# Attention starts with the values' product, and exponential, gelu and the routing's scores are issued later

## The chip, the cores and the metric

The kernel runs on one core of a Trainium2 chip. The metric is the device time of one execution in microseconds. Each engine (TensorE or PE, VectorE or DVE, ScalarE or ACT, GpSimd or POOL, SyncE or SP) takes its own instructions in the order in which the program issued them, so an instruction that waits holds up all that is queued behind it on its engine.

## What is computed

Two residual blocks on 256 tokens of width 2048, all in float32. The first block is a gated MLP with mixing over tokens and then a stick-breaking attention; the second a convolution and mLSTM mixer and then a layer of routed experts (PEER). The change touches the start of the attention and the experts:

```python
def stick_breaking_branch(xn, w_in, w_out):
    proj = xn @ w_in
    q, k, v, zg = jnp.split(proj, 4, axis=-1)
    ...
def peer_ffn(h, wq, keys, u, v):
        q = (xt @ wq).reshape(-1, PEER_HEADS, 2, PEER_HALF)
        s = jnp.einsum('thpc,hpnc->thpn', q, keys)
        sv, si = lax.top_k(s, PEER_TOPK)
        ...
        top_s, top_j = lax.top_k(cand, PEER_TOPK)
        gate = jax.nn.softmax(top_s.astype(jnp.float32), axis=-1)
        act = jax.nn.gelu(jnp.einsum('thkd,td->thk', ue, xt).astype(jnp.float32), approximate=False)
        return jnp.einsum('thk,thkd->td', (gate * act).astype(xt.dtype), ve)
```

The kernel takes the product with all 16384 rows of `u` and of `v`; the routing gives a mostly zero matrix of gates, scattered into DRAM, that the gelu values are multiplied by.

## The kernel before

**Weights.** Every product streams its weights. `Stream` loads 1 MB tiles (`raw`, three buffers, L108, on SP's queue) and splits each half of a tile into a high part `wh` (a copy on ACT, recorded at L194, six buffers) and a low part `wl` (a subtraction on DVE, L131, five buffers). `next` (L147) hands out one half and issues the copies and subtractions that lie some halves ahead. A low part is so issued four halves before TensorE needs it, and a high part five. Here a *half-block* is the TensorE work on one half of a weight tile: 12 matmuls in `gemm` (L328; lines 341 to 343), 8 pairs in `gemm_t` (L379; lines 393 and 395). The stages one after the other are the gated MLP, the attention, the mixer, the products with `wq`, those with `u` (L1283, 32 units of 4 blocks, each block two half-blocks) and those with `v`.

**Background tasks.** All that isn't a large product is written as generators. `bg.step` advances every task to its next `yield`, once per half-block, and `bg.finish` runs named tasks to their end at once. So a `yield` sets the place of an instruction in its engine's order: it moves what follows by one half-block.

**The start of the attention.** `prep` (L612), one task for each quarter of the hidden state, transposes it (L623) and splits it on ACT and DVE (L630). The last quarter's task also works out the reciprocal norm (`rms_rstd`) and then calls `rows` (L597), which spreads it along a row with two small products (diagonals at L601 on DVE, matmuls at L604). `P3` (L245) sets the order of the products: keys, values, queries, gate for the first group. The keys' first block asks for the quarters one by one, the last of them in the middle of its second half-block.

**Routing.** `route` (L1159) runs four times, one after the other, while the `wq` and then the `u` products go on. For each it transposes the queries (L408), copies them on ACT (`qT`, L194), yields twice, and multiplies by the keys (L1172, for `t` 0 and 1); then come two rounds of top-16 on DVE (L1147 to L1151, L1186 to L1205), the subtraction of the maximum (L1210, DVE), the exponential (ACT, with its own table), a yield, the rest of the softmax (L1213 to L1215) and the `scatter` (L1221): 256 indirect DMAs in all on POOL's queue (L1226). The next `route` issues its transposes at the step after the exponential of `t` 1.

**The products with u.** After each block DVE adds the two parts of the accumulator (L1289), and after every second block ACT applies gelu to two of them; after four blocks a DMA on SP writes the unit to DRAM (L1294). `first_v` and `prep_v` (L1257) fetch gates and gelu values of the first units, multiply them (L1263, L1265) and split them for the products with `v` when the last units of `u` run.

Of the kernel before, what the change touches and what calls it, by code (L numbers as in the profile page):

```python
# [8 lines left out]
AF = mybir.ActivationFunctionType  # L9
# [160 lines left out]
def _block(ctx, tc, A, out):  # L170
    nc = tc.nc
# [15 lines left out]
    def act(out, in_, func, **kw):  # L187

        if func not in (AF.Copy, AF.Identity, AF.Abs, AF.Square):
            if func in SETS:  # L190
                table_for(func)
            else:
                table[0] = func
        S.activation(out, in_, func, **kw)  # L194
# [8 lines left out]
    def ft(i, shape, dt=F32):  # L203

        return _view(sb.tile([P, 1024], dt, name=nm(f"f{i}"), tag=f"f{i}"), shape)
# [7 lines left out]
    def rot(group, slots):  # L213
        i = turn.get(group, 0)
        turn[group] = i + 1
        return slots[i % len(slots)]
# [25 lines left out]
                add_w("awo", n, [c - 1])  # L242
    for n in range(4):
        add_w("awo", n, [7])
    P3 = [(w, g) for g in range(2) for w in "kvqz"] + [(w, g) for g in (2, 3) for w in "kvq"] + [("z", 2), ("z", 3)]  # L245
    for w, g in P3:
        add_w("bwi", "qkvz".index(w) * 4 + g, range(4))
    for n in range(4):
# [127 lines left out]
        bg.step()  # L376
        return r

    def gemm_t(x, evac, need=()):  # L379


        acc = pp.tile([P, 512], F32, name=nm("acc"), tag=f"acc{rot('acct', (0, 1))}", bufs=2)
        lo = acc[:, 0:T].rearrange("p (c h) -> p c h", h=2)
        both = acc.rearrange("p (a c h) -> p a c h", a=2, h=2)
        for half in range(2):
            if half:
                bg.step()
            wh, wl = st.next()
            for k in range(8):
                if k % 4 == 0 and need:  # L390
                    bg.finish(need[2 * half + k // 4])
                m = x[half][:, k].rearrange("p (h a c) -> p a c h", h=2, a=2)
                E.matmul(both, wh[:, k * P:(k + 1) * P], m, start=half == 0 and k == 0, stop=False,  # L393
                         skip_group_check=True)
                E.matmul(lo, wl[:, k * P:(k + 1) * P], m[:, 0], start=False, stop=half == 1 and k == 7,  # L395
                         skip_group_check=True)
        evac(acc)
        bg.step()
# [345 lines left out]

    first = True
    for w, g in P3:
        need = [p1tasks[i] for i in range(4)] if first else []
        first = False
        if w == "v":
            d = ft(2, [2, 512])  # L750
            qkv[w, g] = d

            def ev(acc, d=d):
                for t in range(2):
                    V.tensor_scalar(d[:, t], acc[t], r1[:, t:t + 1], None, op0=ALU.mult)
            gemm(x1h, x1l, FULL, ev)
            continue
        d = ft({"q": (0, 0, 0, 3), "k": (1, 1, 1, 6), "z": (3, 6, 0, 1)}[w][g], [4, T])
        for b in range(4):
            def ev(acc, b=b):  # L760
                o = d[:, b].rearrange("p (h c) -> p c h", h=2)
                V.tensor_reduce(o, acc.rearrange("p (a c h) -> p c h a", a=2, h=2),
                                axis=mybir.AxisListType.X, op=ALU.add)
                V.tensor_tensor(d[:, b], d[:, b], rrow[:, 1 if w == "q" else 0], op=ALU.mult)
                if w == "z" and b % 2:
                    act(d[:, b - 1:b + 1], d[:, b - 1:b + 1], AF.Silu)
            gemm_t(xb, ev, need if b == 0 else [])
        if w == "z":
            ytask[g] = bg.add(y3_chain(g, d))
            continue  # L770
        qkv[w, g] = d
        if w == "q":
            atask[g] = bg.add(attn_group(g))
# [385 lines left out]
    def route(n, q, before):  # L1159

        yield from wait(before)
        qT = ft(2, [4, T])

        def dst(pr, p):
            act(qT[:, 2 * pr:2 * pr + 2], p.rearrange("p (k t) -> p k t", k=2), AF.Copy)
        transpose4(lambda t, j: q[:, t, j * P:(j + 1) * P], dst)
        yield
        yield
        for t in range(2):
            p = ps()  # L1170
            for hp in range(4):
                E.matmul(p[:, hp * P:(hp + 1) * P], qT[:, hp, t * P:(t + 1) * P], keysT[:, 4 * n + hp],  # L1172
                         start=True, stop=True)
            s = et(rot("s7", (0, 1)), [4, P])
            act(s, p.rearrange("p (h n) -> p h n", h=4), AF.Copy)
            yield
            ws = ft(rot("rw", (3, 6)), [1024])
            sv = ws[:, 0:64].rearrange("p (a b) -> p a b", a=4)
            si = ws[:, 64:128].bitcast(U32).rearrange("p (a b) -> p a b", a=4)
            sif = ws[:, 128:192].rearrange("p (a b) -> p a b", a=4)  # L1180
            yield from paced([op for hp in range(4) for op in topk16(s[:, hp], sv[:, hp], si[:, hp])], 4)
            V.tensor_copy(sif, si)
            for hh in range(2):
                head = 2 * n + hh
                cand = et(rot("cand", (2, 3)), [16, 16])
                V.tensor_tensor(cand, sv[:, 2 * hh][:, :, None].to_broadcast([P, 16, 16]),  # L1186
                                sv[:, 2 * hh + 1][:, None, :].to_broadcast([P, 16, 16]), op=ALU.add)
                wo = 256 + hh * 256
                tj = ws[:, wo + 16:wo + 32].bitcast(U32)
                yield from paced(topk16(cand.rearrange("p a b -> p (a b)"), tvs[:, t, head], tj), 2)  # L1190
                ab = ws[:, wo + 32:wo + 64].bitcast(U32).rearrange("p (a b) -> p a b", a=2)
                V.tensor_scalar(ab[:, 0], tj, 4, None, op0=ALU.logical_shift_right)
                V.tensor_scalar(ab[:, 1], tj, 15, None, op0=ALU.bitwise_and)
                abf = ws[:, wo + 64:wo + 96].rearrange("p (a b) -> p a b", a=2)
                key = ws[:, wo + 96:wo + 128].rearrange("p (a b) -> p a b", a=2)
                V.tensor_copy(abf, ab)
                for s_ in range(2):
                    oh = et(rot("oh", (4, 5)), [16, 16])
                    V.tensor_tensor(oh, abf[:, s_][:, :, None].to_broadcast([P, 16, 16]),
                                    C("iota")[:, None, 0:16].to_broadcast([P, 16, 16]), op=ALU.is_equal)  # L1200
                    V.tensor_tensor(oh, oh, sif[:, 2 * hh + s_][:, None, :].to_broadcast([P, 16, 16]),  # L1201
                                    op=ALU.mult)
                    V.tensor_reduce(key[:, s_], oh, axis=mybir.AxisListType.X, op=ALU.add)
                V.scalar_tensor_tensor(key[:, 0], key[:, 1], float(P), key[:, 0], op0=ALU.mult, op1=ALU.add)
                V.tensor_scalar(idx[:, t, head * 16:(head + 1) * 16], key[:, 0], float(P), C("pidx"),  # L1205
                                op0=ALU.mult, op1=ALU.add)
                yield
            hs = slice(2 * n, 2 * n + 2)
            ex, es = gat[:, t, hs], ws[:, 192:194]
            V.tensor_tensor(ex, tvs[:, t, hs], tvs[:, t, hs, 0:1].to_broadcast([P, 2, 16]), op=ALU.subtract)  # L1210
            act(ex, ex, AF.Exp)
            yield
            V.tensor_reduce(es, ex, axis=mybir.AxisListType.X, op=ALU.add)  # L1213
            V.reciprocal(es, es)
            V.tensor_tensor(ex, ex, es[:, :, None].to_broadcast([P, 2, 16]), op=ALU.mult)  # L1215
            if n == 0:
                scatter(n, [t])
        if n:
            scatter(n, range(2))
# [53 lines left out]
    def first_v():  # L1273
        yield from wait(rts[-1])
        while len(done_u) < NU - 4:
            yield
        load_v(0)
        while len(done_u) < NU - 1:
            yield
        load_v(1)  # L1280
        yield from prep_v(0)

    done_u = set()  # L1283
    fv = bg.add(first_v())
    for u in range(NU):
        a = ft(rot("act", (0, 1)), [4, T])
        for b in range(4):
            def ev(acc, b=b):
                V.tensor_reduce(a[:, b].rearrange("p (h c) -> p c h", h=2),  # L1289
                                acc.rearrange("p (a c h) -> p c h a", a=2, h=2), axis=mybir.AxisListType.X, op=ALU.add)  # L1290
                if b % 2:
                    act(a[:, b - 1:b + 1], a[:, b - 1:b + 1], AF.Gelu)
            gemm_t(x3, ev)
        nc.sync.dma_start(out=Ad[u], in_=a)  # L1294
        done_u.add(u)
    bg.finish(fv)
    bg.drain()

# [135 lines left out]
```

## Time and profile before

| | us |
|---|---|
| median of 3 runs (3077.58 to 3080.34) | 3079.38 |
| the profiled execution | 3076.71 |
| its span in the profile | 3074.9 |
| PE busy in it | 3007.0 (98%) |
| DVE busy | 2028.9 (66%) |
| ACT busy | 1469.3 (48%) |
| POOL busy | 471.8 (15%) |

The profile names for each instruction its engine, line, and output and input tiles; an idle stretch before it is put down to the instruction that ended it. The granted clock is TensorE's, as a share of full speed. Idle time of TensorE is what the span could lose; idle time of another engine matters only where TensorE waits for it.

### The profile page before, as it was taken

The numbers are of one execution on the slowest core, as the hardware profiler recorded it, in microseconds if no ns is written. First come the engines' busy times: TensorE is split into PE (matmuls) and PEld (weight loads), VectorE is DVE, ScalarE is ACT, GpSimd is POOL, SyncE is SP. The second block draws the span as 40 slices with busy tenths as digits, with TensorE's granted clock in tenths as the row PEclk, the third lists the DMA queues.
The fourth block names the chain that finished last, engine by engine and source line by source line (L and its number), as shares of the span: only waits on it lengthen the run. The fifth ranks groups of instructions, "written<-read, shape, count | busy, mean of one in ns | idle before, by whom it ended". The sixth has DMA issues, their size and how long they took to land.

```text
span 3074.9 us, 39571 instructions
## 1 busy us (share of the span) xinstructions
PE 3007.0 (98%) x15488; PEld 2670.8 (87%) x15488; DVE 2028.9 (66%) x2704; ACT 1469.3 (48%) x1622; POOL 471.8 (15%) x275
## 2 busy tenths in 40 slices
PE   8999999998999999999999999999999999999997
PEld 7888888887999987888888888899999888888886
DVE  6565556666666676656558999855556766666666
ACT  5454444444554555545444444544444444444443
POOL 0000000000000000000001668888830000000001
PEclk9999999999999999999999999999999999999999
DMA  7776666665666575666656677878776988888874
GB/s 276 246 255 214 219 221 216 225 211 188 195 200 206 190 247 194 203 205 207 229 187 206 185 198 201 235 226 232 222 252 237 320 275 274 283 286 287 272 259 153
DMA packets 230603, 702.33 MB, mean 228 GB/s; under 512 B 50576, under 2 KB 144912, under 8 KB 158864
## 3 DMA queue, kind: packets, MB, share of 16 engines
q1 hardware_dynamic: 192912, 697.57, 66.7%
q0 software_dynamic: 37504, 2.25, 2.8%
q8 instruction: 121, 1.98, 0.2%
q14 instruction: 66, 0.54, 0.1%
HBM read 647.18 MB, written 52.56 MB: 228 GB/s over the span
## 4 chain that ended last, share of the span: by engine, by line
PE 88%; DVE 8%; ACT 2%; issue 1%; DMA 0%; SPq 0%; DVEq 0%; ACTq 0%
PE acc L393 16%; PE acc L341 13%; PE acc L342 13%; PE acc L343 13%; PE acc L395 8%; PE y L343 7%; PE y L342 7%; PE y L341 7%; DVE wl L131 3%; ACT e L194 1%; DVE f L1289 0%; PE ms L562 0%; PE ms L408 0%; DVE f L1151 0%; DVE e L1201 0%
## 5 line engine op out<-in xcount | busy, mean ns | idle before, releaser
L131 DVE TENSOR_TENSOR wl<-raw,wh 128x1024 fp32r<-128x1024 f32 x1106 | 1342.0, 1221 | 600.6 <-PE acc L342 262.9
L194 ACT ACTIVATE wh<-raw 128x1024 fp32r<-128x1024 f32 x1106 | 1159.8, 1056 | 1157.2 <-PE acc L343 511.5
L393 PE MATMUL acc<-xs,wh 128*128 128x512 f32 x2816 | 932.5, 385 | 0.0
L395 PE MATMUL acc<-xs,wl 128*128 128x256 f32 x2816 | 770.0, 273 | 3.5 <-DVE wl L131 3.5
L1226 POOL DMA_INDIRECT Gd<-f x256 | 455.5, 1779 | 1795.5 <-DVE f L1215 1672.3
L341 PE MATMUL acc<-wh,xs 128*128 128x512 f32 x1728 | 664.3, 384 | 13.4 <-ACT wh L194 9.3
L342 PE MATMUL acc<-wl,xs 128*128 128x512 f32 x1728 | 657.3, 380 | 0.5 <-DVE wl L131 0.5
L343 PE MATMUL acc<-wh,xs 128*128 128x512 f32 x1728 | 657.0, 380 | 0.0
L393 PEld LDWEIGHTS acc<-xs,wh 128*128 128x128 f32 x2816 | 535.1, 190 | 74.5 <-DVE xs L630 0.2
L395 PEld LDWEIGHTS acc<-xs,wl 128*128 128x128 f32 x2816 | 543.1, 193 | 4.2 <-DVE wl L131 4.1
L341 PE MATMUL y<-wh,xs 128*128 128x512 f32 x1024 | 388.1, 379 | 0.0
L342 PE MATMUL y<-wl,xs 128*128 128x512 f32 x1024 | 388.1, 379 | 0.0
L343 PE MATMUL y<-wh,xs 128*128 128x512 f32 x1024 | 388.1, 379 | 0.0
L341 PEld LDWEIGHTS acc<-wh,xs 128*128 128x128 f32 x1728 | 328.1, 190 | 62.9 <-ACT wh L194 9.3
L343 PEld LDWEIGHTS acc<-wh,xs 128*128 128x128 f32 x1728 | 327.8, 190 | 47.1 <-DVE xs L837 0.4
L342 PEld LDWEIGHTS acc<-wl,xs 128*128 128x128 f32 x1728 | 328.2, 190 | 46.7 <-DVE wl L131 1.0
L343 PEld LDWEIGHTS y<-wh,xs 128*128 128x128 f32 x1024 | 193.5, 189 | 27.5
L341 PEld LDWEIGHTS y<-wh,xs 128*128 128x128 f32 x1024 | 193.5, 189 | 27.5
L342 PEld LDWEIGHTS y<-wl,xs 128*128 128x128 f32 x1024 | 193.5, 189 | 27.4
L1289 DVE TENSOR_REDUCE f<-acc 128x256 f32<-128x512 f32 x128 | 88.5, 691 | 107.7 <-PE acc L395 107.6
L194 ACT ACTIVATE f<-f 128x512 f32<-128x512 f32 (+1 forms) x80 | 47.2, 591 | 225.0 <-DVE f L1289 162.4
L1314 POOL TENSOR_TENSOR res<-res,xs 128x512 f32<-128x512 f32 x6 | 9.7, 1645 | 801.0 <-DVE res L1311 801.0
(219 smaller groups left out, 1715.8 us busy)
## 6 DMA issues: line engine op xcount, KB each, us to landing
raw<-in_pu_dram SPq DMA_DIRECT2D x128, 1024.0 KB, 4.9
raw<-in_pv_dram SPq DMA_DIRECT2D x128, 1024.0 KB, 5.4
raw<-in_bwi_dram SPq DMA_DIRECT2D x64, 1024.0 KB, 4.9
raw<-in_w_dram SPq DMA_DIRECT2D x56, 1024.0 KB, 5.4
Gd<-zero SPq DMA_DIRECT2D x64, 512.0 KB, 6.9
raw<-in_aw_u_dram SPq DMA_DIRECT2D x32, 1024.0 KB, 5.7
raw<-in_aw_z_dram SPq DMA_DIRECT2D x32, 1024.0 KB, 5.8
raw<-in_awo_dram SPq DMA_DIRECT2D x32, 1024.0 KB, 5.8
```

The costliest lines, as they stand in the source:

```text
L131: self.nc.vector.tensor_tensor(l, raw[:, j * 1024:(j + 1) * 1024], self.hi[q].bitcast(F32), op=ALU.subtract)
L194: S.activation(out, in_, func, **kw)
L341: E.matmul(o, a, wa, start=first and opens, stop=False)
L342: E.matmul(o, a, wb, start=False, stop=False)
L343: E.matmul(o, b, wa, start=False, stop=fin and closes)
L393: E.matmul(both, wh[:, k * P:(k + 1) * P], m, start=half == 0 and k == 0, stop=False, skip_group_check=True)
L395: E.matmul(lo, wl[:, k * P:(k + 1) * P], m[:, 0], start=False, stop=half == 1 and k == 7, skip_group_check=True)
L1226: nc.gpsimd.indirect_dma_start(out=Gd[t][hh].rearrange("e c -> (e c)")[:, None], out_offset=bass.IndirectOffsetOnAxis(ap=idx[:, t, at:at + ...
L1289: V.tensor_reduce(a[:, b].rearrange("p (h c) -> p c h", h=2), acc.rearrange("p (a c h) -> p c h a", a=2, h=2), axis=mybir.AxisListType.X, ...
L1314: (nc.gpsimd if t == 0 or n in (1, 2) else V).tensor_tensor(v, v, gb[1][:, (n - 1) * 512:n * 512], op=ALU.add)
```

## The change

Three edits. First, in group 0 the values' product comes before the keys', and as it is a `gemm`, each quarter of the hidden state is asked for a quarter of that product (two half-blocks) later than the one before. Second, in the routing four yields instead of two stand between the copies of `qT` and the first scores, and five yields between the subtraction L1210 and the exponential. Third, in the products with `u` each gelu is held back and issued at the end of the next block, ahead of that block's own addition; the DMA that stores the unit and the mark that the unit is done go with the last one.

```diff
-    P3 = [(w, g) for g in range(2) for w in "kvqz"] + [(w, g) for g in (2, 3) for w in "kvq"] + [("z", 2), ("z", 3)]
+    P3 = [(w, 0) for w in "vkqz"] + [(w, 1) for w in "kvqz"] + [(w, g) for g in (2, 3) for w in "kvq"] + [("z", 2), ("z", 3)]
...
-                if k % 4 == 0 and need:
-                    bg.finish(need[2 * half + k // 4])
...
-        need = [p1tasks[i] for i in range(4)] if first else []
+        need = {i: [p1tasks[i]] for i in range(4)} if first else {}
...
-            gemm(x1h, x1l, FULL, ev)
+            gemm(x1h, x1l, FULL, ev, need)
...
-            gemm_t(xb, ev, need if b == 0 else [])
+            gemm_t(xb, ev)
...
         transpose4(lambda t, j: q[:, t, j * P:(j + 1) * P], dst)
-        yield
-        yield
+        for _ in range(4):
+            yield
...
             V.tensor_tensor(ex, tvs[:, t, hs], tvs[:, t, hs, 0:1].to_broadcast([P, 2, 16]), op=ALU.subtract)
+            for _ in range(5):
+                yield
             act(ex, ex, AF.Exp)
...
+    owed = []
+
+    def settle():
+        while owed:
+            owed.pop(0)()
+
     for u in range(NU):
         a = ft(rot("act", (0, 1)), [4, T])
+
+        def leave(u=u, a=a):
+            act(a[:, 2:4], a[:, 2:4], AF.Gelu)
+            nc.sync.dma_start(out=Ad[u], in_=a)
+            done_u.add(u)
+
         for b in range(4):
-            def ev(acc, b=b):
+            def ev(acc, b=b, a=a, leave=leave):
+                settle()
                 V.tensor_reduce(a[:, b].rearrange("p (h c) -> p c h", h=2),
                                 acc.rearrange("p (a c h) -> p c h a", a=2, h=2), axis=mybir.AxisListType.X, op=ALU.add)
-                if b % 2:
-                    act(a[:, b - 1:b + 1], a[:, b - 1:b + 1], AF.Gelu)
+                if b == 1:
+                    owed.append(lambda: act(a[:, 0:2], a[:, 0:2], AF.Gelu))
+                elif b == 3:
+                    owed.append(leave)
             gemm_t(x3, ev)
-        nc.sync.dma_start(out=Ad[u], in_=a)
-        done_u.add(u)
+    settle()
     bg.finish(fv)
     bg.drain()
```

## Rows read from the trace of the kernel before

**Rows 1.** TensorE's waits, whole span: waiter, its releaser: us in total, times, longest.
```profile
PE ms L1172 <- ACT f L194: 14.5, 3, 5.2
...
PE ms L604 <- DVE e L601: 7.6, 1, 7.6
...
PE acc L395 <- DVE wl L131: 3.5, 2, 1.8
```

**Rows 2.** Stretches: bounds, length, PE, PEld, DVE, ACT, POOL busy, clock, DMA, GB/s.
```profile
1690.00:1960.00 270.00, 252.04 (x1521) 230.82 (x1519) 251.87 (x638) 123.49 (x141) 198.29 (x113) 0.97 0.71 197
1960.00:2395.00 435.00, 435.00 (x2656) 400.07 (x2657) 262.17 (x262) 202.78 (x214) 253.23 (x147) 1.00 0.78 238
2395.00:3050.00 655.00, 655.00 (x3036) 573.58 (x3035) 417.71 (x357) 296.28 (x284) 0.00 (x0) 1.00 0.80 274
```

**Rows 3.** The same view, the stretches right after TensorE's four long idle times.
```profile
1715.20:1720.40 5.20, 5.17 (x19) 4.72 (x20) 3.69 (x8) 3.79 (x5) 3.62 (x3) 0.50 0.76 208
...
1798.60:1802.30 3.70, 3.70 (x15) 3.43 (x16) 2.31 (x3) 3.70 (x5) 1.67 (x2) 0.54 1.00 324
...
1881.20:1884.30 3.10, 3.09 (x12) 2.91 (x13) 1.68 (x2) 3.10 (x5) 2.79 (x2) 0.51 0.75 217
...
715.30:720.30 5.00, 5.00 (x17) 4.45 (x18) 1.16 (x4) 1.72 (x3) 0.00 (x0) 0.50 0.06 23
```

**Rows 4.** Timeline, DVE and PE, start of the attention: start, duration, instruction, [idle before].
```profile
710.28 1.22 DVE L131 TENSOR_TENSOR wl<-raw,wh 128x1024 fp32r<-128x1024 f32 x1
...
714.87 0.48 DVE L601 TENSOR_SCALAR e<-con,rstd 128x128 f32<-128x128 f32 x2
...
715.30 1.19 PE L604 MATMUL ms<-e,con 128*128 128x128 f32 x4 [7.59 <-DVE e L601]
```

**Rows 5.** ScalarE's waits from 1640 to 1960 us.
```profile
ACT f L194 <- DVE f L1289: 68.2, 15, 7.8
...
ACT f L194 <- DVE f L1210: 43.7, 7, 12.9
```

**Rows 6.** Timeline of the first stall in the routing, PE, DVE and ACT.
```profile
1703.78 1.04 PE L408 MATMUL ms<-con,xs 128*128 128x128 f32 x8
...
1711.35 0.19 DVE L1210 TENSOR_TENSOR f<-f 128x32 f32<-128x32 f32 x1
...
1711.57 0.23 ACT L194 ACTIVATE f<-f 128x32 f32<-128x32 f32 x1 [12.87 <-DVE f L1210]
...
1712.77 1.28 ACT L194 ACT_TABLE_LOAD   x1
...
1714.60 1.07 ACT L194 ACTIVATE f<-ms 128x512 f32<-128x512 f32 x2
1715.23 2.07 PE L1172 MATMUL ms<-phaseA,f 128*128 128x128 f32 x8 [5.17 <-ACT f L194]
```

**Rows 7.** Timeline, an exponential's place on PE and its operand on DVE.
```profile
1752.77 1.06 PE L1172 MATMUL ms<-phaseA,f 128*128 128x128 f32 x8
...
1756.77 0.18 DVE L1210 TENSOR_TENSOR f<-f 128x32 f32<-128x32 f32 x1
```

**Rows 8.** Stretch after the routing, DVE alone: length, busy (instructions), clock, DMA, GB/s.
```profile
1980.00:2060.00 80.00, 46.11 (x46) 1.00 0.80 229
```

**Rows 9.** SP's waits, whole span: the store of a unit for its gelu.
```profile
SPq L1294 <- ACT f L194: 61.2, 32, 2.4
```

**Rows 10.** Stretches, the scatters (L1226) alone: length, POOL busy (count), clock, DMA, GB/s.
```profile
1673.00:1835.00 162.00, 104.10 (x60) 0.97 0.70 201
...
1990.00:2250.00 260.00, 222.18 (x125) 1.00 0.80 226
```

**Rows 11.** The slowest 40 us of POOL, same columns.
```profile
1740.00:1780.00 40.00, 24.29 (x14) 1.00 0.72 205
```

**Rows 12.** Timeline, DVE at the end of the products with u.
```profile
2375.77 1.22 DVE L1263 TENSOR_TENSOR f<-f,f 128x1024 f32<-128x1024 f32 x1
...
2395.40 0.69 DVE L1289 TENSOR_REDUCE f<-acc 128x256 f32<-128x512 f32 x1
```

More of the change, by code (lines that the diff above doesn't have):

```diff
@@ L377, in gemm, with gemm_t @@
         return r
-    def gemm_t(x, evac, need=()):
+    def gemm_t(x, evac):
         acc = pp.tile([P, 512], F32, name=nm("acc"), tag=f"acc{rot('acct', (0, 1))}", bufs=2)
```

## The prediction

> **What bounds the kernel now.** I read the waits of TensorE first, because the stretches show it busy without a gap outside a few places: 435 of 435 us and 655 of 655 us in two long stages [rows 2]. Only its idle time, and time at a low clock, can be won. The reader is to see that three of its waits [rows 1] lie in the places that the change touches: 7.6 us for the spread norm at the start of the attention (L604 for L601), 14.5 us in three waits for the routing's scores (L1172 for ACT), and 3.5 us for two low parts (L395 for L131). The last two kinds are the 18.0 us that PE is idle from 1690 to 1960 us, 270 - 252.0 [rows 2]. Then I read the clock right after each long wait. It is near 0.5, the 1.2 GHz level, for 5.17, 3.70 and 3.09 us of busy time after the three waits in the routing and for 5.0 us after the one in the attention [rows 3]. Work at that level takes twice as long, so what is lost is busy time x (1 - clock): 2.6 + 1.7 + 1.5 = 5.8 us in the routing and 2.5 us in the attention. Waits and clock together are 7.6 + 2.5 = 10.1 us in the attention and 18.0 + 5.8 = 23.8 us in the routing.
>
> Last I looked for the cause of the long waits. In the routing ACT itself is blocked: it stands 43.7 us at exponentials that wait for L1210 and 68.2 us at gelus that wait for L1289 [rows 5]. The timeline of the first stall shows how this reaches PE: the transposes run on PE at 1703.78, but ACT stands for 12.87 us before an exponential whose operand DVE delivers at 1711.35; a table load and a gelu follow, the copies of qT run at 1714.60 and the scores at 1715.23, 5.17 us late [rows 6].
>
> DVE lags behind PE. The exponential is issued one half-block before the transposes. A half-block is 2.6 us: 435 / (2656 / 16), or 12 x 655 / 3036 for the other kind [rows 2]. So PE was at its place at about 1701.2, and DVE reached L1210 10.2 us later [rows 6]. After one half (t 0) of a routing the scores of t 1 are what comes one half-block behind, and the lag is 1756.77 - (1752.77 - 2.6) = 6.6 us [rows 7]. DVE is busy 251.9 of 270 us there [rows 2].
>
> **The change part by part.** *Values first.* Nothing is added. The last quarter's task needs three steps, of which the third holds the rows' matmuls. Before, they are forced after 1.5 half-blocks of the keys' product; now ordinary steps issue them after 3, ahead of the force. PE has 1.5 x 2.6 = 3.9 us more work in front of them. But one more low part is issued ahead of L601 on DVE, which costs 1.2 us (the one at 710.28) [rows 4]. The wait of 7.59 us becomes 7.6 - 3.9 + 1.2 = 4.9 us. That is still long, so I expect the low clock again, with PE resuming about 1.2 us later inside the same low stretch: 0.6 us less lost. The gain is 2.7 + 0.6, taken as 3 us. Its bounds are 0 (L601 slips by all that is won) and the whole 10.1 us. The values' evacuation needs the norm only after eight half-blocks, so it can't wait. The keys move by eight half-blocks with their evacuation, and queries and attention keep their place.
>
> *Exponential five steps later.* L1210 stays where it is, so at the place of the exponential it was issued 5 x 2.6 = 13 us earlier, more than even the old lag of 10.2 us. ACT should not stand there. The softmax's tail, the scatters, the second scores and the next routing are all issued later with it. On DVE the tail L1213 now waits for an exponential one half-block old; ACT needs a table load (1.28 us) and 0.23 us for it [rows 6], under 2.6 us. One more pair of table loads appears, since the second exponential of the first routing now falls behind a gelu: 2.6 us on ACT, which is busy 123 of 270 us [rows 2]; hidden.
>
> *Scores two steps later.* The copies of qT get 4 x 2.6 = 10.4 us instead of 5.2. In front of them on ACT can stand two table loads, a gelu and high parts, about 5 us; covered unless ACT is blocked again.
>
> *Gelu one block later.* It is issued 5.2 us after its last addition. With a lag of 6 to 8 us ACT may still stand 1 to 3 us at it; six buffered high parts and the 10.4 us for qT cover that. The store of the unit moves on SP's queue with it, past one weight load. SP stands there 61.2 / 32 = 1.9 us each time now [rows 9]; a gelu whose operand is ready can only shorten that. The two buffers of the unit are reused two units later, so the store has ample time.
>
> *What pays for DVE's lag.* DVE's work is not reduced, so removing ACT's blocks alone would turn the waits into waits for low parts. A low part is issued four half-blocks, 10.4 us, ahead; less its own 1.2 us, PE starves once the lag exceeds about 9 us, and the 10.2 us above is over it. The twelve new steps per routing (2 + 5 + 5) are what lets DVE catch up: without routing it is busy 46.1 of 80 us [rows 8], so a half-block leaves 2.6 x 0.42 = 1.1 us. Five steps pay back 5.5 of the 6.6 us built up for one t, and the two ahead of the scores the rest. I expect the lag to peak near 7 us, at about 8 in the first routing, which shares DVE with the residual's scaling. That is a narrow margin to 9. So I take all 18.0 us of waits and 5.8 us of clock as won, 23.8 us, with bounds of 0 and 23.8.
>
> *What moves to the end.* Four routings last 48 half-blocks longer, 125 us, less the stalls. They end near 2060 us, well inside the u stage that ends at 2395 [rows 12]. On POOL the scatters start some 13 us later (seven more steps, 18 us, with DVE less late). The first 64 of them run at 162 / 60 = 2.70 us each, later ones at 260 / 125 = 2.08 [rows 10]; 64 x 2.70 + 192 x 2.08 = 572 us after about 1686 they end near 2258, and the gates are first needed at 2375.8 before [rows 12], at about 2353 in the new time. The first units' preparation moves by one step at most, and its last split stays where it was, behind the last gelu; the products with v need that part two half-blocks later. I cost both at nothing.
>
> **Sum.** 3 + 23.8 = 26.8 us. The profiled execution took 3076.71, so 3049.9 for it; it lies 2.7 us under the median, and 3079.4 - 26.8 = 3052.6 us is the forecast for the median.
>
> **Rivals.** (a) *DVE is the bound and the waits change their name.* For it: 251.9 of 270 us busy. Against it: 1.1 us of room in each added half-block. If the room pays only half, some 12 us of the routing's gain are lost to waits of L395 for L131: 3079.4 - 3 - 12 = 3064. (b) *The norm is hidden altogether*, because DVE has less in front of L601 than I count: 7 us more, 3045. Against it: the chain to L601 is DVE's own work and only 3.9 us are moved ahead of it. (c) *The edits in ACT's order don't do what they say*, because the copies of qT wait behind high parts and not behind a blocked exponential: little more than the 3.5 us and some clock are won, 3072. The 12.87 us row speaks against it [rows 6]. (d) *Slower: the scatters come late.* They now run mainly beside DVE's routing work, and the slowest 40 us hold 14, 2.86 us each [rows 11]. If all ran so, they would end at 1686 + 732 = 2418, 65 us after the gates are needed; DVE would stand, and PE after the 10 us of low parts in hand: 55 us, 3108. It decides from a mean of about 2.75 us per scatter, where the 26.8 us are used up. Against it: the slow pace belongs to the first routing, whose scatters go to only two of the four gate tensors and wait for each other, and one scatter itself takes 104.1 / 60 = 1.74 us beside a dense DVE and 222.2 / 125 = 1.78 us later [rows 10]. The Trainium skill (page "SBUF — State Buffer", section "Who interferes with whom") says that a DVE instruction with two inputs in SBUF contends with a GpSimd instruction that reads SBUF, and that the later one blocks; by that rule the longer routing would stretch the scatters and (d) would gain weight. The trace does not bear it out: a scatter is no longer beside the dense DVE.
>
> **How the numbers follow.** Forecast 0.72, (a) 0.12, (b) 0.06, (c) 0.05, (d) 0.03, other 0.02. The forecast's own spread is 3046 to 3060: the first part's bounds and a few microseconds of lag. The range takes in most of (a) and touches (b): 3045 to 3065. Faster by over 0.2% (6 us, about what a measurement of this kernel can tell from no change) holds the forecast, (a), (b) and most of (c): 0.93. Same 0.04, slower 0.03.
>
> **What would show it.** In the trace after, TensorE's waits at L1172 and at L395 should be gone or under 2 us in all, and no stretch of low clock left between 1690 and 2060 us. ACT's total at L1210 should be near 0 and at L1289 in that stretch under 25 us. L604 should still wait 4 to 6 us. The last scatter should start near 2260 us. Waits of L395 for L131 in place of L1172's would mean (a); waits of DVE's L1263 for POOL's gathers, (d). The prediction is wrong if PE's idle time in the routing falls and the span does not.

## The result and the profile after

The changed kernel takes 3050.6 us in the median (3049.15 to 3051.16), against 3078.7 us for the kernel before in the same comparison: a ratio of 0.991 (0.989 to 0.9925), or 28.1 us less. Forecast were 3052.6 us and a gain of 26.8. The profiled execution took 3051.16 us, its span is 3049.4, which is 25.5 us less than the span before; without the 1.3 us by which its wait at the kernel's start is longer (below) it would be 26.8.

The waits of TensorE over the whole span, after (waiter, releaser: us in total, times, longest; the lines have moved by two, L604 is now L602, L1172 L1170 and L395 L393):

```profile
PE acc L341 <- ACT wh L194: 10.6, 1, 10.6
PE ms L814 <- DVE res L805: 9.2, 2, 5.4
PE ms L602 <- DVE e L599: 4.9, 1, 4.9
PE acc L341 <- ACT xs L194: 4.2, 3, 2.1
```

Of the three waits that the change aimed at [rows 1], those for the routing's scores and for low parts are gone altogether, and the one for the spread norm fell from 7.6 to 4.9 us. The others lie in the kernel's first 60 us and in the layer norms; the change doesn't touch them (the first, at the start, is 10.6 us in this one execution and was 9.3).

The stretches after (bounds and length, then busy us of PE, PEld, DVE, ACT and POOL with their instructions, granted clock, DMA share, GB/s):

```profile
718.40:723.00 4.60, 4.60 (x13) 3.87 (x14) 1.16 (x2) 1.60 (x3) 0.00 (x0) 0.50 0.51 167
...
1690.00:1960.00 270.00, 270.00 (x1671) 248.78 (x1670) 239.22 (x533) 139.19 (x154) 177.51 (x98) 1.00 0.75 221
...
1980.00:2060.00 80.00, 80.00 (x493) 73.63 (x493) 73.42 (x160) 40.64 (x44) 66.91 (x36) 1.00 0.79 228
```

Where TensorE was busy for 252.0 of 270 us at a mean clock of 0.97 [rows 2], it is now busy all the time at 1.00. DVE has 12.7 us less to do in that stretch, 239.2 against 251.9 us, and more behind it: 73.4 of 80 us where it had 46.1 [rows 8]. The routing's work has been spread, not shortened. Of the places that the change touches only that of the norm still shows the low clock, 0.50 for at least 4.6 us.

### The profile page after: what moved, and what is told of

Same layout as the page of the kernel before. It is cut to its first block, busy times and chain, and to the rows that moved or that the text cites. A ratio compares the mean times of both kernels' runs of the same rounds, so it can differ in the third digit from the quotient of the medians.

```text
span 3049.4 us, 39564 instructions
## 1 busy us (share of the span) xinstructions
PE 3000.9 (98%) x15488; PEld 2666.0 (87%) x15488; DVE 2028.3 (67%) x2704; ACT 1475.4 (48%) x1624; POOL 481.7 (16%) x275
## 4 chain that ended last, share of the span: by engine, by line
PE 73%; DVE 2%; ACT 1%; issue 0%; DVEq 0%; ACTq 0%
PE acc L391 19%; PE acc L393 10%; PE y L343 7%; PE y L341 7%; PE y L342 7%; PE acc L341 7%; PE acc L342 7%; PE acc L343 7%; ACT e L194 1%; DVE wl L131 1%; PE ms L406 0%; DVE res L1325 0%; ACT L184 0%; PE ms L1170 0%; PE ms L814 0%
## 5 line engine op out<-in xcount | busy, mean ns | idle before, releaser
L393 PE MATMUL acc<-xs,wl 128*128 128x256 f32 x2816 | 767.6, 273 | 0.0
L1226 POOL DMA_INDIRECT Gd<-f x256 | 465.4, 1818 | 1836.9 <-DMA xs<-in_rows_dram 1683.3
L341 PE MATMUL acc<-wh,xs 128*128 128x512 f32 x1728 | 666.0, 385 | 14.7 <-ACT wh L194 10.6
L391 PEld LDWEIGHTS acc<-xs,wh 128*128 128x128 f32 x2816 | 532.3, 189 | 73.4
L393 PEld LDWEIGHTS acc<-xs,wl 128*128 128x128 f32 x2816 | 540.7, 192 | 0.1
L341 PEld LDWEIGHTS acc<-wh,xs 128*128 128x128 f32 x1728 | 329.0, 190 | 64.5 <-ACT wh L194 10.6
L1302 DVE TENSOR_REDUCE f<-acc 128x256 f32<-128x512 f32 x128 | 88.3, 690 | 92.2 <-PE acc L393 66.9
L341 PE MATMUL acc<-wh,f 128*128 128x512 f32 x256 | 98.0, 383 | 0.0
```

Source lines behind the costliest of these rows:

```text
L341: E.matmul(o, a, wa, start=first and opens, stop=False)
L1226: nc.gpsimd.indirect_dma_start(out=Gd[t][hh].rearrange("e c -> (e c)")[:, None], out_offset=bass.IndirectOffsetOnAxis(ap=idx[:, t, at:at + ...
```

## The experiments

Times are medians. "Gain" is against the kernel before in the same comparison, which took 3078.9, 3077.8 and 3078.4 us for the runs 1 to 4, 5 to 8 and 9 to 11. Beside the changed kernel it took 3078.7, so where a run is set against the changed kernel's 3050.6 us, up to 0.9 us of the distance can be the comparison's; the gains are free of that (the changed kernel's is 28.1).

| run | us | ratio to before (interval) | gain |
|---|---|---|---|
| 1, values first alone | 3075.8 | 0.999 (0.9981 to 0.9999) | 3.1 |
| 2, five steps ahead of the exponential alone | 3052.7 | 0.9914 (0.9899 to 0.9929) | 26.2 |
| 3, two more steps ahead of the scores alone | 3066.8 | 0.9958 (0.9944 to 0.9972) | 12.1 |
| 4, later gelu alone | 3070.2 | 0.997 (0.9958 to 0.9982) | 8.7 |
| 5, changed kernel, the five steps behind the exponential | 3049.4 | 0.9907 (0.9892 to 0.9923) | 28.4 |
| 6, changed kernel, exponential in a side task, no added steps | 3063.9 | 0.9955 (0.9941 to 0.9968) | 13.9 |
| 7, changed kernel, norm's spread two steps later | 3045.4 | 0.9898 (0.9882 to 0.9913) | 32.3 |
| 8, changed kernel without the later gelu | 3049.1 | 0.9906 (0.9891 to 0.9921) | 28.7 |
| 9, changed kernel, norm's spread cut in two | 3042.6 | 0.9886 (0.987 to 0.9901) | 35.8 |
| 10, as 9, with the five steps as the routing's only edit | 3042.3 | 0.9883 (0.9868 to 0.9898) | 36.1 |
| 11, as 8, with two steps for the exponential and two for the scores | 3055.4 | 0.9925 (0.9912 to 0.9939) | 23.0 |

Two theories stand against each other. One is that freeing ACT is enough: the exponential and the gelus block it, so the copies of qT come late. The other is that DVE's lag has to be paid with added half-blocks, and that a blocked ACT costs nothing by itself.

### 1. Values first alone

The hunks of the diff on `P3`, `gemm_t` and `need`, and nothing else.

> The first edit alone: values before keys in the first group, the quarters asked for one by one; routing and gelu as before. By my sum: 3 us gained (about 3076 us), the wait of L604's matmuls for L601 down from 7.6 to 4.9 us, the low clock after it shorter. If the norm were hidden or the edit idle: 10 us or 0. The three waits for the scores stay at 14.5 us.

The gain is 3.1 us (interval 0.3 to 5.8) and the wait for the norm 4.9 us, as in the changed kernel. The span of the profiled execution is 1.9 us shorter than before. The waits for scores and low parts are those of before:

```profile
PE ms L1170 <- ACT f L194: 14.6, 3, 5.3
...
PE ms L602 <- DVE e L599: 4.9, 1, 4.9
...
PE acc L393 <- DVE wl L131: 3.5, 2, 1.8
```

### 2. Five steps ahead of the exponential alone

```diff
+            for _ in range(5):
+                yield
             act(ex, ex, AF.Exp)
```

> The five steps ahead of the exponential alone, two steps ahead of the scores, gelu and values as before. If the blocked exponential and the lag of DVE are the cause: the waits for the scores fall from 14.5 to under 3 us and those for low parts from 3.5 to under 1.5, so 18 to 22 us gained (about 3058 to 3061). If the gelus alone can still block ACT ahead of qT (they keep their place): one or two waits of 2 to 4 us stay, 12 to 16 us gained.

It gains 26.2 us (interval 22 to 31), more than the 18 to 22 expected here; the span of the profiled execution is 23.9 us shorter, close to the 23.8 us that the prediction counted in the routing. The gelus stayed where they were and blocked ACT for longer than before, 98.0 us against 87.8 in the same stretch (1640 to 2070 us), and TensorE did not wait once in the routing. ACT's waits at gelus in this kernel and in the kernel before, then the stretch in this kernel:

```profile
ACT f L194 <- DVE f L1291: 98.0, 26, 8.3
```

```profile
ACT f L194 <- DVE f L1289: 87.8, 25, 7.8
```

```profile
1690.00:1960.00 270.00, 270.00 (x1668) 248.75 (x1667) 243.56 (x560) 138.43 (x154) 189.19 (x104) 1.00 0.76 219
```

So the second expectation, that gelus ahead of qT could still hold TensorE up, falls.

### 3. Two more steps ahead of the scores alone

```diff
-        yield
-        yield
+        for _ in range(4):
+            yield
```

> The two extra steps ahead of the scores alone. The copies of qT get 10.4 us instead of 5.2, about the 10.9 us from the transposes' end to the copies' end in the first stall. By ACT's blocks alone: all waits for the scores gone, 14.5 us and 5.8 us of clock, about 20 us gained (3059). By my reading, in which DVE's lag has to be paid: only 2 x 1.1 us of room per routing are added, so waits of L395 for low parts rise from 3.5 to some 6 to 10 us, and 10 to 15 us are gained (3064 to 3069).

12.1 us gained, inside the second theory's 10 to 15 and well below the first's 20. No wait for the scores is left, but the waits for low parts have risen from 3.5 us in 2 places to 8.2 in 7. TensorE's wait in this kernel:

```profile
PE acc L395 <- DVE wl L131: 8.2, 7, 2.3
```

The copies of qT in time are therefore not enough: waits for low parts take the place of part of those for the scores. In this run DVE itself stood 3.5 us for high parts from ACT between 1690 and 1960 us, so some of the 8.2 us may still have come through ACT; run 6 tells the two apart.

### 4. The later gelu alone

The hunk of the diff on the loop over `u`, and nothing else.

> The later gelu alone. The exponential still blocks ACT ahead of qT; what falls away between the two is one table load and one gelu, 1.9 us in each of three stalls. Expected: the waits for the scores fall from 14.5 to 8 to 10 us and 5 to 7 us are gained (about 3073). If the gelus' 68 us of blocked ACT were what stops TensorE: 15 us or more. If gelu has no part in it: 0.

The waits for the scores fall to 9.0 us as expected, those for low parts rise a little, and 8.7 us are gained instead of 5 to 7 (interval 5.5 to 12.9; the span of the profiled execution is 6.2 us shorter). TensorE's waits in this kernel, and the stretch:

```profile
PE ms L1172 <- ACT f L194: 9.0, 3, 3.3
...
PE acc L395 <- DVE wl L131: 4.3, 3, 2.3
```

```profile
1690.00:1960.00 270.00, 256.73 (x1559) 234.75 (x1558) 258.80 (x649) 130.63 (x148) 190.73 (x104) 0.99 0.73 202
```

4.7 us less idle (13.3 against 18.0) and a mean clock of 0.99 against 0.97 [rows 2]: that shorter waits also save clock was not in my figure. Whether the rest is more than noise the interval can't say. ACT's 68 us at gelus were not what stopped TensorE, or the gain would be far larger.

### 5. The five steps behind the exponential

```diff
-            for _ in range(5):
-                yield
             act(ex, ex, AF.Exp)
+            for _ in range(5):
+                yield
```

> The changed kernel with the five steps moved behind the exponential: it is issued right after its subtraction L1210 again, and blocks ACT for as long as DVE lags (6 to 7 us, eight times), but the transposes and qT come five half-blocks later. If the place of the exponential is what counts: waits for the scores come back, 5 us or more, and the time is 3058 or longer. By my reading (room for DVE and distance to qT count, and six buffered high parts cover a blocked ACT): no wait for the scores, within 2 us of the changed kernel (3050.6), though ACT stands 40 us or more at exponentials.

The time is that of the changed kernel, 3049.4 us, with ACT blocked at the exponentials for 48.5 us, as much as before the change (49.3 in the same stretch, 1640 to 2070 us). TensorE is busy for the whole stretch. ACT's wait and the stretch in this kernel:

```profile
ACT f L194 <- DVE f L1208: 48.5, 8, 7.0
```

```profile
1690.00:1960.00 270.00, 270.00 (x1671) 248.81 (x1671) 239.25 (x537) 137.38 (x152) 182.17 (x99) 1.00 0.77 222
```

With the later gelu and the two steps ahead of the scores in place, it does not matter that the exponential is issued later. What matters is that the five steps are there. No run has the steps behind the exponential without those two edits.

### 6. ACT free, but no added room

```diff
-            for _ in range(5):
-                yield
-            act(ex, ex, AF.Exp)
-            yield
-            V.tensor_reduce(es, ex, axis=mybir.AxisListType.X, op=ALU.add)
...
+            softs.append(bg.add(soft(n, t, ex, es)))
+            yield
...
+    def soft(n, t, ex, es):
+        for _ in range(5):
+            yield
+        act(ex, ex, AF.Exp)
+        yield
+        V.tensor_reduce(es, ex, axis=mybir.AxisListType.X, op=ALU.add)
...
```

`soft` holds the rest of the tail and the scatters too; the steps ahead of the scores are two again.

> The changed kernel with the exponential, its tail and its scatters in a task of their own that starts five steps after the subtraction, while the routing goes on at once, and two steps ahead of the scores: ACT is as free as in the changed kernel, but a routing again takes 28 half-blocks, as before, so DVE gets no added room. If freeing ACT is enough: 3050 to 3052, no waits of TensorE in the routing. If DVE's lag has to be paid with room (my sum): waits for low parts take the place of the waits for scores, 5 to 15 us in all, 3056 to 3066.

3063.9 us, 13.3 more than the changed kernel (14.2 by the gains). ACT never waits for an exponential's operand, no score is late, and yet TensorE is idle for 12.0 us in the stretch, all of it behind low parts. DVE made those low parts late by itself: in the stretch it stood only 1.2 us for ACT's high parts. TensorE's wait, DVE's wait from 1690 to 1960 us and the stretch in this kernel:

```profile
PE acc L393 <- DVE wl L131: 12.0, 12, 2.3
```

```profile
DVE wl L131 <- ACT wh L194: 1.2, 2, 1.0
```

```profile
1690.00:1960.00 270.00, 258.02 (x1582) 234.91 (x1581) 260.08 (x645) 134.12 (x150) 185.36 (x102) 1.00 0.73 208
```

DVE is busy 260.1 of 270 us, more than in any other run. Its lag can be read here as in the prediction: in the third routing's second half the subtraction runs at 1866.99, and its place on TensorE is one half-block ahead of the transposes at 1858.74, a lag of 10.9 us, above the 9 from which by the forecast low parts come late, and they do. PE and DVE in this kernel:

```profile
1858.74 1.04 PE L406 MATMUL ms<-con,xs 128*128 128x128 f32 x8
...
1866.99 0.18 DVE L1208 TENSOR_TENSOR f<-f 128x32 f32<-128x32 f32 x1
```

Together with run 5 this settles the cause: with room and an ACT blocked at exponentials nothing is lost, and with an ACT that stands at no exponential and no room half the gain is lost.

### 7. The spread of the norm two steps later

```diff
                 rms_rstd(x1["rstd"], st1)
-                yield
+                for _ in range(3):
+                    yield
                 rows(x1["rstd"])
```

> The changed kernel with two more steps ahead of the spread of the norm, so that its matmuls are issued after five half-blocks of the values' product and not after three. DVE's diagonals came 4.9 us after TensorE asked; 5.2 us more work stand in front now. Expected: the wait under 0.5 us and no low clock after it, 4.9 + about 2 us gained: 3043 to 3045. If the diagonals slip with it on DVE (two more low parts ahead of them, 2.4 us): a wait of 2 us stays, 3046 to 3048.

3045.4 us, 5.1 less than the changed kernel (4.2 by the gains), just under the 3046 to 3048 of the second expectation, whose mechanism it is: a wait of 2.0 us is left, and on DVE three low parts, not one, now stand in front of the diagonals. No low clock follows that wait. TensorE's wait, DVE's timeline and the stretch around it in this kernel:

```profile
PE ms L602 <- DVE e L599: 2.0, 1, 2.0
```

```profile
715.15 3.49 DVE L131 TENSOR_TENSOR wl<-raw,wh 128x1024 fp32r<-128x1024 f32 x3
...
718.55 0.48 DVE L599 TENSOR_SCALAR e<-con,rstd 128x128 f32<-128x128 f32 x2
```

```profile
715.00:725.00 10.00, 8.03 (x40) 6.80 (x39) 6.63 (x10) 5.02 (x8) 0.00 (x0) 1.00 0.73 242
```

### 8. The changed kernel without the later gelu

The hunk on the loop over `u` taken back.

> The changed kernel with gelu at its old place. If the room for DVE and the later exponential and scores do the work: no wait of TensorE in the routing, within 1.5 us of the changed kernel (3050.6). If the later gelu is needed: waits for the scores of 2 us or more, 3054 or longer. ACT should stand at L1289 longer than in the changed kernel either way.

3049.1 us, no different from 3050.6, with ACT blocked at gelus for 102.7 us (1640 to 2070 us), against 9.4 with the later gelu. Both rows, this kernel's first and the changed kernel's (1640 to 2060 us) second:

```profile
ACT f L194 <- DVE f L1289: 102.7, 27, 8.3
```

```profile
ACT f L194 <- DVE f L1302: 9.4, 7, 2.7
```

The later gelu does just what it says and is worth nothing beside the steps.

### 9. The spread cut in two

```diff
             V.tensor_scalar(dg[:, t], ident, r[:, t:t + 1], None, op0=ALU.mult)
+        for _ in range(3):
+            yield
         p = ps()
...
                 rms_rstd(x1["rstd"], st1)
-                yield
-                rows(x1["rstd"])
+                yield from rows(x1["rstd"])
```

> The changed kernel with the spread of the norm cut in two: DVE's diagonals are issued right behind the norm, ahead of the next low part, and their matmuls two steps later than in the changed kernel. With the two steps alone 2.0 us of wait stayed, since two more low parts slipped ahead of the diagonals. If that is why: no wait of TensorE there, 2 us gained over that run, about 3043.5; and 7 us over the changed kernel. If the 2.0 us come from the norm's own chain: the wait stays and the time is 3045.5.

3042.6 us: the wait is gone, and 8.0 us are gained over the changed kernel (7.7 by the gains). DVE's diagonals and TensorE's matmuls in this kernel:

```profile
714.67 0.48 DVE L599 TENSOR_SCALAR e<-con,rstd 128x128 f32<-128x128 f32 x2
...
716.26 0.61 PE L604 MATMUL ms<-e,con 128*128 128x128 f32 x4
```

### 10. The lean kernel

Run 9 with the hunks on gelu and on the scores taken back.

> The same with gelu at its old place and two steps ahead of the scores as before, so that of the routing's edits only the five steps ahead of the exponential are left: ten half-blocks per routing and not twelve. From the run with that edit alone: no wait of TensorE in the routing, within 1.5 us of the kernel with all edits and the split (about 3043.5). If the two other edits are needed once the rest is faster: waits for scores or low parts of 2 us or more, 3046 or longer.

3042.3 us, the best of all, with ten added half-blocks per routing and not twelve; TensorE is busy for 270.00 of the 270 us. Of the three edits in the routing and in the products with u, two can be left out: the scores' two steps and the later gelu.

### 11. Two steps instead of five

```diff
-            for _ in range(5):
+            for _ in range(2):
                 yield
             act(ex, ex, AF.Exp)
```

on run 8's kernel, with two steps ahead of the scores.

> The lean kernel's routing with two steps ahead of the exponential instead of five, scores at two steps, gelu at its old place, values first with the spread whole. Four half-blocks of room per routing, 4.4 us, against the 10 us that DVE's lag grew by in a routing of before. If room is what counts: waits of 2 to 8 us come back, of either kind, and the time is 3053 to 3059 (the changed kernel: 3050.6). If two steps are as good as five: no waits, 3050.

3055.4 us, and waits of both kinds are back, 4.9 us in all, which is the distance to the changed kernel:

```profile
PE acc L393 <- DVE wl L131: 3.2, 4, 1.5
PE ms L1170 <- ACT f L194: 1.7, 3, 0.6
```

So four half-blocks of room per routing buy most of the gain, and ten (run 10) all of it. Across the runs TensorE's idle time in the routing falls as the room grows: 18.0 us before and 12.0 in run 6 with no added half-block per routing, 8.2 with two (run 3), 4.9 with four, none with ten.

## Why the prediction was right, point by point

*The sum.* 3 us for the values and 23.8 for the routing were forecast; run 1 gave 3.1 and run 2 26.2, whose interval (22 to 31 us) holds the 23.8. Their sum, 29.3, is the whole change (28.1) within its interval. The spans of the profiled executions add up more closely: 1.9 + 23.9 = 25.8, for 25.5.

*The norm.* The sum of 7.6 - 3.9 + 1.2 = 4.9 us was met: 4.87 us after, below. The one low part that now stands in front of the diagonals is there as well. The 0.6 us of clock did not come: the low clock after the wait lasts at least 4.6 us (the stretch from 718.40 above), about as long as the 5.0 before [rows 3], and was forecast 1.2 us shorter. Run 1 is too coarse to show a difference that small in the time. Timeline after, DVE and PE:

```profile
716.81 1.22 DVE L131 TENSOR_TENSOR wl<-raw,wh 128x1024 fp32r<-128x1024 f32 x1
717.95 0.48 DVE L599 TENSOR_SCALAR e<-con,rstd 128x128 f32<-128x128 f32 x2
...
718.37 1.19 PE L602 MATMUL ms<-e,con 128*128 128x128 f32 x4 [4.87 <-DVE e L599]
```

*What pays for DVE's lag.* This step carried the forecast, and runs 5, 6 and 11 bear it out. The size holds too: in the first routing's second half the subtraction runs at 1724.11, and its place on TensorE is six half-blocks of 2.6 us ahead of the transposes at 1732.47, so at 1716.9: a lag of 7.2 us where I had put about 8, below the 9 from which TensorE starves. Timeline after, DVE, PE and ACT:

```profile
1724.11 0.18 DVE L1208 TENSOR_TENSOR f<-f 128x32 f32<-128x32 f32 x1
...
1732.47 1.04 PE L406 MATMUL ms<-con,xs 128*128 128x128 f32 x8
...
1733.50 0.23 ACT L194 ACTIVATE f<-f 128x32 f32<-128x32 f32 x1
```

The pay-back was put too low. By the forecast five steps pay back 5.5 of 6.6 us and the two ahead of the scores the rest. In run 10 the two are not there, and the lag still doesn't grow: in its second routing TensorE reaches what is issued six half-blocks after the subtraction 9.1 us after DVE runs it, in the first half (the scores) as in the second (the transposes), which is a lag of 15.6 - 9.1 = 6.5 us both times. DVE and PE in run 10:

```profile
1763.29 0.18 DVE L1209 TENSOR_TENSOR f<-f 128x32 f32<-128x32 f32 x1
...
1772.41 1.06 PE L1171 MATMUL ms<-phaseA,f 128*128 128x128 f32 x8
...
1811.36 0.18 DVE L1209 TENSOR_TENSOR f<-f 128x32 f32<-128x32 f32 x1
...
1820.46 1.04 PE L406 MATMUL ms<-con,xs 128*128 128x128 f32 x8
```

*The exponential, the scores, the gelu.* Here the steps were right in what they say of ACT (it stands 9.4 us at L1302, forecast under 25, and not at all at L1208) and wrong in the weight they gave it. I took all three as needed to free ACT and the room as what keeps the waits from coming back under another name. Run 5 shows that ACT need not be freed, run 8 that the gelu's place is worth nothing beside the steps, run 10 that the scores' two steps aren't needed either.

*Rival (a)*, that the waits change their name, is what run 6 and run 3 show where the room is missing: 12.0 and 8.2 us at low parts. The change escapes it because its delays are steps. *Rival (b)* did not come about by this change; run 7 brought most of it and run 9 all of it; by the gains they were worth 4.2 and 7.7 us, where I had put 7. *Rival (c)* is refuted by run 2.

*The scatters.* This is the term that was off. I put their end at 2258 us; the last one starts at 2301.7. The first 64 took 195 us, 3.0 each, and not 2.70, and they waited 73.4 us for each other's transfers; later ones took 280 / 129 = 2.17 each and not 2.08. After, the stretches with the scatters alone (length, POOL busy, clock, DMA, GB/s) and who held up the first 64:

```profile
1685.00:1880.00 195.00, 112.43 (x64) 1.00 0.73 222
...
2020.00:2300.00 280.00, 231.62 (x129) 1.00 0.83 231
```

```profile
DMA Gd<-f: 73.4, 33
```

It cost nothing, since the gates were first needed at 2354.3 (forecast 2353; 2375.8 less the 26.8 of the sum would be 2349, and the forecast does not say where the rest comes from). The mean pace was (2301.7 - 1684.4) / 255 = 2.42 us, and rival (d) decides from 2.75. One scatter itself is still 112.4 / 64 = 1.76 us, so the added time lies in the waits for transfers and not in POOL's own work; why they grew is open, no run varied them.

## What to carry to other kernels

Where an engine beside the bottleneck is nearly full, its lag is the quantity to follow: count what is issued on it per step of the bottleneck against what a step leaves free, and compare the lag with how far ahead its results are issued. The wait that the profile names (here ACT, blocked behind an exponential) can be only the place where that lag surfaces first; taking that wait away without adding room moves it to another line (runs 3 and 6), and spreading the same work over more steps removes it, with the steps ahead of the exponential (run 2) or behind it (run 5, beside two other edits). For a short chain in front of the bottleneck, issue its first half at once and its last half later, so that other work of the same engine doesn't slip in between (run 9 against run 7).

## What the runs showed of the hardware that was not expected

ACT can stand blocked for some 100 us of 430 (runs 2 and 8) without a single wait of TensorE in the routing. Six buffered high parts are what should cover it, but no run varied their number. A stall that is made shorter can give back more than its length, when the low clock after it goes as well: run 7 took 2.9 us off a wait, left the clock at 1.00, and gained 4.2 us. It need not: values first took 2.7 us off the same wait, and the low clock behind the remaining 4.9 us lasted about as long as before. And the scatters' pace changes by a tenth, from 2.70 to 3.0 us each for the first 64, while one scatter's time on POOL stays at 1.7 to 1.8 us.
